# A decoder layer's feed-forwards: a seven-product scheme with other signs, and two of its four weight sums made by transfers that add

## The chip, the cores and the metric

The kernel runs on one core of one Trainium2 chip. The core has a matrix engine (PE), a vector engine (DVE), a scalar engine (ACT), a general engine (POOL) and a queue engine (SP) that starts transfers; each works through its own list of instructions in order, and they wait for one another by semaphores. The metric is device time in microseconds, the median of three runs.

## The reference, cut to what matters

The layer is a chain of a feed-forward, a token mixer (attention beside a convolution), a second feed-forward and a gated embedding. S is 512 tokens, the model width is 1024, the feed-forward's width 2816. What the change touches is `swiglu`, which is called twice:

```
def swiglu(h, w_gu, w_down):
    g, u = jnp.split(h @ w_gu, 2, axis=-1)
    return (jax.nn.silu(g) * u) @ w_down
...
x = x + 0.5 * swiglu(rmsnorm(x, ffn1_norm[i]), ffn1_wgu[i], ffn1_wdown[i])
...
x = x + 0.5 * swiglu(rmsnorm(x, ffn2_norm[i]), ffn2_wgu[i], ffn2_wdown[i])
```

All of it is in 32-bit floats.

## The kernel before, in words

**Products.** Activations are held feature by feature (128 partitions, 512 tokens). Every 32-bit operand is split into a high part (`hi`, made on ACT) and the rest (`lo`, on DVE: source minus high part), and a product is three matmuls (`mm3`): hi times hi, lo times hi, hi times lo. A weight piece is 128x1024 (512 KB).

**Feed-forward.** The 2816 hidden features are 22 columns of 128. The first columns of each feed-forward (4 in the first, 2 in the second, `plain`) are done in the plain way with 512-token matmuls. The other columns are taken two at a time (`pair`): 9 pairs in the first, 10 in the second, 19 in all. A pair is a 2x2 block product (two columns f, two halves kh of the model width, two halves of the tokens), and it is done by a scheme of seven block products instead of eight, once for the gate (g) and once for the up half (u): 14 products of 12 matmuls of 256 tokens. The scheme needs four sums or differences of the token halves, made once for a feed-forward (`sums`, tiles `f_t`), and four sums of the pair's weight blocks (`sm[0]` to `sm[3]`, tiles `f_s`), made for every pair. Blocks are named by f and kh: `A[0,0]`, `A[0,1]`, `A[1,0]`, `A[1,1]`. Each weight sum is two additions of 128x512, so a pair has eight. The products are called in the order 1 and 2, 6 and 5, 7 and 3, 4: 1, 2 and 4 use blocks as loaded, 3, 5, 6 and 7 use sums. After every 8 columns (and at the end) the down projection runs: 8 groups (`f_d`) of 18 or 24 matmuls of 512 tokens. So the pairs stand in six rows: 4 and 6; 8 to 14; 16 to 20 in the first feed-forward, 2 to 6; 8 to 14; 16 to 20 in the second.

**Buffers.** Loaded weights go to 3 buffers (`raw`), and `A[1,1]` to one of 2 more (`k`); high and low parts go to 3 buffers each (`hi`, `lo`). In the first feed-forward (`own`) the high and low parts of a sum have general tiles of their own.

**What sets the order.** The program is first recorded as a list of operations without times. A planner (`costs`, `deadlines`, `simulate`, `plan`) then gives each a cost, walks through them with the buffers it has, and writes one fixed list of instructions for each engine. The additions of the sums are `flex`: the planner puts each on POOL or on DVE. POOL and DVE lock each other out over additions of two tiles (`op.lock`). All instructions are issued by one line (L1522 before), so the profile is read by tile names: `raw_wgu` a loaded piece, `whi_wgu` and `wlo_wgu` its parts, `f_wh` and `f_wl` the parts of a sum with its own tile, `f_s` a sum, `f_g8b`, `f_u8a` the accumulators of pair 8, `f_gs`, `f_us`, `f_gc`, `f_uc` what is read out of them, `f_n_rb` the norm's factor, `f_n_sp` the matmul that makes it.

Of the kernel before, what the change touches and what calls it, by code (L numbers as in the profile page):

```python
# [20 lines left out]
KD = D // P  # L21
# [205 lines left out]
class Program:  # L227
# [69 lines left out]
    def costs(self, op, eng=None):  # L297
# [32 lines left out]
        elif op.what == "dma_start" and eng == "ACT":  # L330
            op.cost, op.lat = 0.5, 2.6
        elif eng == "ACT":
            op.cost, op.lat = 0.07 + n * 0.88e-3, 0.17
            op.cost += 0.094 * vecs
            if "accum_out" in op.k:
                op.cost += 0.1
            f = op.a[2].name if len(op.a) > 2 else "Copy"
            op.fset = SETS.get(f)
        elif eng == "POOL":
            op.lat = 0.15  # L340
            if op.what == "tensor_tensor":
# [25 lines left out]
def deadlines(prog, when):  # L367
# [5 lines left out]
    for op in reversed(prog.ops):  # L373
# [9 lines left out]
        for s in op.succs:  # L383
            d = s.ls
            if s.preds[op] and not s.eng == op.eng == "PE":
                d -= op.lat + (1.8 + op.dma if op.eng == "SP" else 0.0)
            ls = min(ls, d - op.cost)
# [8 lines left out]
def simulate(prog, slots):  # L396
# [64 lines left out]
    def launch(op, t):  # L461
# [19 lines left out]
        if op.eng == "SP":  # L481
            dma_free = max(t + 0.6, dma_free) + op.dma
            op.end = dma_free + 1.5
        else:
            op.end = t + c + op.lat
# [166 lines left out]
def record():  # L652
# [242 lines left out]
    def sums(tag, gain):  # L895
# [4 lines left out]
        t1, t2 = slice(0, HS), slice(HS, S)  # L900
        forms = [[] for _ in range(4)]
        for q in range(KD // 4):
            vs = [ftile(f"{tag}_t{f}_{q}") for f in range(4)]
            for j in range(2):
                k, v = 2 * q + j, [t[:, j * HS : (j + 1) * HS] for t in vs]
                g1, g2 = gain[:, k : k + 1], gain[:, k + 4 : k + 5]
                nc.gpsimd.tensor_tensor(v[0], x[k][:, t2], x[k][:, t1], op=ALU.subtract)
                nc.scalar.activation(v[0], v[0], AF.Copy, scale=g1)
                nc.scalar.activation(v[2], x[k][:, t2], AF.Copy, scale=g1)
                for to, xs, less in ((2, t2, 2), (1, t2, 0), (3, t1, 1)):  # L910
                    nc.vector.scalar_tensor_tensor(
                        v[to], x[k + 4][:, xs], g2, v[less], op0=ALU.mult, op1=ALU.subtract
                    )
# [6 lines left out]
    def ffn(tag, wgu, wdown, h, gain, ss, after, cuts, wide, plain, own):  # L920
# [8 lines left out]

        def act_split(i, u):  # L930
            c, q = i // CH, i % CH // 4
            if (c, q) not in quads:
                quads[c, q] = [nc.tile(f"{tag}_a{c}{q}{p}", [P, 4, S], F32R, "o") for p in "hl"]
            acts[i] = [t[:, i % 4] for t in quads[c, q]]
            split_into(acts[i][0], acts[i][1], u)

# [29 lines left out]
        def pair(i, T, new):  # L966

            A = {}
            for f in range(2):
                for kh in range(2):  # L970
                    A[f, kh] = nc.tile(f"raw_{wgu}{i}_{f}{kh}", [P, PIECE], F32, "k" if f == kh == 1 else "raw")
            sm = [[ftile(f"{tag}_s{n}_{i}_{c}") for c in range(2)] for n in range(4)]

# [4 lines left out]

            def add(n, a, b, op):
                for c in range(2):  # L980
                    s = slice(c * S, (c + 1) * S)
                    ab = [v[c] if isinstance(v, list) else v[:, s] for v in (a, b)]
                    nc.flex.tensor_tensor(sm[n][c], *ab, op=op)

# [17 lines left out]
            for f, kh in ((0, 0), (0, 1), (1, 0), (1, 1)):  # L1002
                load(f, kh)
            add(0, A[1, 0], A[1, 1], ALU.add)
            add(1, sm[0], A[0, 0], ALU.subtract)
            add(3, A[0, 1], sm[1], ALU.subtract)
            add(2, A[0, 0], A[1, 0], ALU.subtract)
            quarter = lambda k0, t: [(h[k][0][:, t], h[k][1][:, t]) for k in range(k0, k0 + 4)]
# [15 lines left out]
            def both(n1, s1, r1, n2, s2, r2, first):  # L1024
                w1, w2 = form(n1, s1), form(n2, s2)
                for m in range(2):
                    times(m, n1, w1, r1, b2, first)
# [3 lines left out]
            for m in both(1, A[0, 0], quarter(0, lo_), 2, A[0, 1], quarter(4, lo_), True):  # L1031
# [3 lines left out]
                if m == 0:  # L1035
                    nc.vector.tensor_tensor(to, to if new else b1[m], rb[:, lo_], op=ALU.mult)
            for m in both(6, sm[1], T[1], 5, sm[0], T[0], False):
                nc.scalar.copy(U[m][:, lo_], b2[m])
                nc.scalar.copy(U[m][:, hi_], b1[m])
            for m in both(7, sm[2], T[2], 3, sm[3], quarter(4, hi_), False):  # L1040
                nc.vector.tensor_tensor((g, u)[m][1][:, hi_], b2[m], U[m][:, hi_], op=ALU.add)
# [11 lines left out]
            nc.vector.tensor_tensor(g[1][:, lo_], b2[0], rb[:, lo_], op=ALU.mult)  # L1053
            nc.scalar.activation(g[1], g[1], AF.Silu)
            nc.vector.tensor_tensor(u[1][:, hi_], u[1][:, hi_], g[1][:, hi_], op=ALU.mult)
            nc.vector.tensor_tensor(u[1][:, lo_], b2[1], g[1][:, lo_], op=ALU.mult)
            act_split(i + 1, u[1])

# [563 lines left out]
```

## Time and profile before

| | |
|---|---|
| three runs | 1172.52, 1174.57, 1174.89 us; median 1174.57 |
| the profiled execution, first to last instruction (span) | 1172.4 us |
| PE busy | 1161.6 us, 99% of the span, granted clock 0.999 |
| DVE, ACT, POOL busy | 973.4, 639.7, 456.2 us |
| HBM read | 112.04 MB |

The profile is of one execution, whose own time the page gives as its span; the median of the runs is 2.2 us above it. Its page has the busy time of each engine, the span in 40 slices, the chain of work that ended last, and groups of instructions with what their engine waited for just before. In a group `out<-in`, the number after x is how many, then the sum, the mean in ns and the idle time before. Where a query gives windows or tiles, times are in us from the span's start.

### The profile page before, as it was taken

To read this page: it belongs to the slowest core of one execution; us is meant where nothing else is said; L and a number is where in the kernel's file an instruction comes from. 1 tells how busy PE (TensorE), PEld (TensorE's weight loads), DVE (VectorE), ACT (ScalarE), POOL (GpSimd) and SP (SyncE) were. 2 spreads that over 40 slices of the span, in tenths; PEclk is the share of its full clock that TensorE was granted. 3 is DMA by queue.
4 is the path that set the end of the run, shared out by engine and by line. 5 is a ranking of instruction groups with operands and counts; after the bars stand their busy time and mean duration, and the time that the engine had idled before them with its cause. 6 is when DMAs were issued, how large, how long until landed. Compare 5 with 4: busy or idle time off the path is not lost.

```text
span 1172.4 us, 17962 instructions
## 1 busy us (share of the span) xinstructions
PE 1161.6 (99%) x6740; PEld 1029.6 (88%) x6740; DVE 973.4 (83%) x1481; ACT 639.7 (55%) x1139; POOL 456.2 (39%) x418
## 2 busy tenths in 40 slices
PE   9999999999999999999999999999999999999998
PEld 7898899889988888878888888889988999899886
DVE  8995799679886898999999786678966997599885
ACT  8552455335545579979865573545541555245542
POOL 2430465033303987887898600104402440122000
PEclk9999999999999999999999999999999999999999
DMA  7422323342233221312223233332333223331331
GB/s 226 146 85 96 126 75 106 99 136 76 82 104 100 90 91 37 108 55 72 76 89 106 88 94 93 105 96 102 107 104 132 74 86 100 121 127 41 104 108 72
DMA packets 37815, 115.30 MB, mean 98 GB/s; under 512 B 4704, under 2 KB 9440, under 8 KB 37728
## 3 DMA queue, kind: packets, MB, share of 16 engines
q1 hardware_dynamic: 37584, 114.12, 31.0%
q8 instruction: 53, 0.87, 0.3%
q14 instruction: 34, 0.28, 0.1%
q10 hardware_dynamic: 144, 0.03, 0.0%
HBM read 112.04 MB, written 2.10 MB: 97 GB/s over the span
## 4 chain that ended last, share of the span: by engine, by line
PE 94%; ACT 2%; DVE 2%; POOL 1%; issue 1%; DMA 0%; SPq 0%; DVEq 0%; ACTq 0%
PE f_d L1522 20%; PE ap L1522 4%; PE ga L1522 4%; PE pg L1522 4%; PE cp L1522 4%; PE wo L1522 4%; PE ca L1522 3%; PE gb L1522 3%; PE cb L1522 3%; PE f_u L1522 2%; PE f_g L1522 2%; PE q1b L1522 2%; PE q0b L1522 2%; PE sc L1522 2%; PE f_u14b L1522 1%; PE f_u20b L1522 1%
## 5 line engine op out<-in xcount | busy, mean ns | idle before, releaser
L1522 POOL TENSOR_TENSOR f_s<-raw_wgu,raw_wgu 128x512 f32<-128x512 f32 x51 | 86.6, 1710 | 345.5 <-DMA raw_wgu<-in_wgu 115.6
L1522 POOL TENSOR_TENSOR y<-y,ct 128x507 f32<-128x507 f32 (+27 forms) x90 | 119.1, 1343 | 6.2 <-ACT ct L1522 4.6
L1522 ACT ACTIVATE whi_wgu<-raw_wgu 128x1024 fp32r<-128x1024 f32 (+1 forms) x93 | 76.2, 834 | 81.5 <-PE f_d L1522 29.5
L1522 DVE TENSOR_TENSOR wlo_wgu<-raw_wgu,whi_wgu 128x1024 fp32r<-128x1024 f32 (+1 forms) x93 | 105.1, 1140 | 7.8 <-ACT whi_wgu L1522 7.3
L1522 DVE SCALAR_TENSOR_TENSOR cz<-u,dww,cz 128x504 f32<-128x504 f32 (+25 forms) x145 | 104.7, 732 | 2.3
L1522 ACT ACTIVATE whi_wd<-raw_wd 128x1024 fp32r<-128x1024 f32 (+1 forms) x48 | 47.4, 987 | 103.9 <-PE f_d L1522 84.6
L1522 DVE TENSOR_TENSOR f_d<-f_d,f_n_rb 128x512 f32<-128x512 f32 x48 | 33.4, 697 | 75.8 <-PE f_d L1522 75.8
L1522 DVE TENSOR_TENSOR f_wl<-f_s,f_wh 128x512 fp32r<-128x512 f32 x72 | 71.4, 1012 | 1.5 <-ACT f_wh L1522 1.0
L1522 POOL TENSOR_TENSOR f_s<-raw_wgu,f_s 128x512 f32<-128x512 f32 x31 | 52.3, 1694 | 51.6 <-DVE f_us L1522 20.6
L1522 DVE TENSOR_TENSOR wlo_wgu<-f_s,whi_wgu 128x512 fp32r<-128x512 f32 x80 | 66.3, 863 | 6.0 <-ACT whi_wgu L1522 5.8
L1522 ACT ACTIVATE whi_wgu<-f_s 128x512 fp32r<-128x512 f32 x80 | 46.6, 625 | 32.4 <-PE f_d L1522 8.9
L1522 ACT ACTIVATE ct<-u,dww 128x505 f32<-128x505 f32 (+28 forms) x90 | 58.2, 701 | 2.2 <-DVE u L1522 2.1
L1522 ACT ACTIVATE f_wh<-f_s 128x512 fp32r<-128x512 f32 x72 | 43.6, 626 | 26.6 <-DVE f_s L1522 12.9
L1522 POOL TENSOR_TENSOR f_s<-f_s,raw_wgu 128x512 f32<-128x512 f32 x31 | 49.2, 1594 | 20.8 <-DVE f_s L1522 6.0
L1522 DVE TENSOR_TENSOR wlo_wd<-raw_wd,whi_wd 128x1024 fp32r<-128x1024 f32 (+1 forms) x48 | 54.1, 1128 | 3.8 <-ACT whi_wd L1522 3.6
L1522 ACT ACTIVATE f_gs<-f_gs 128x512 f32<-128x512 f32 x44 | 27.6, 629 | 34.8 <-DVE f_gs L1522 34.4
L1522 POOL TENSOR_TENSOR f_t<-x 128x256 f32<-128x256 f32 x8 | 6.5, 807 | 86.8 <-DVE x L1522 81.6
L1522 DVE SCALAR_TENSOR_TENSOR x<-f_d,x 128x512 f32<-128x512 f32 x48 | 32.9, 689 | 1.4
L1522 DVE TENSOR_TENSOR f_s<-raw_wgu,raw_wgu 128x512 f32<-128x512 f32 x25 | 32.9, 1319 | 0.0
L1522 ACT ACTIVATE s<-s,m,q_r 128x128 f32<-128x128 f32 x64 | 31.0, 491 | 0.5 <-DVE m L1522 0.4
L1522 ACT ACTIVATE whi_wzc<-raw_wzc 128x1024 fp32r<-128x1024 f32 x16 | 17.0, 1061 | 22.3 <-issue 8.4
L1522 ACT ACTIVATE whi_wzg<-raw_wzg 128x1024 fp32r<-128x1024 f32 x16 | 17.1, 1069 | 16.9 <-PE ga L1522 5.0
(1621 smaller groups left out, 4525.3 us busy)
## 6 DMA issues: line engine op xcount, KB each, us to landing
raw_wgu<-in_wgu SPq DMA_DIRECT2D x80, 512.0 KB, 3.7
raw_wd<-in_wd SPq DMA_DIRECT2D x32, 512.0 KB, 3.5
raw_wzc<-in_wzc SPq DMA_DIRECT2D x16, 512.0 KB, 3.6
raw_wzg<-in_wzg SPq DMA_DIRECT2D x16, 512.0 KB, 3.6
raw_wd<-in_wd SPq DMA_DIRECT2D x16, 384.0 KB, 3.1
raw_wgu<-in_wgu SPq DMA_DIRECT2D x32, 128.0 KB, 2.9
raw_wq<-in_wq SPq DMA_DIRECT2D x8, 512.0 KB, 3.6
raw_wap<-in_wap SPq DMA_DIRECT2D x8, 512.0 KB, 3.6
```

What stands on the lines that cost most here:

```text
L1522: getattr(engines[op.eng], op.what)(*a, **k)
```

## The change

The scheme of seven products is written with other signs, so that every sum of weights is an addition. Two of a pair's four sums are then made by a transfer from HBM that adds to what lies in the buffer (`landed`): `A[1,0]` has `A[1,1]` added to it, and later, when product 1 has its parts and the first sum has been read, `A[0,0]` has `A[1,0]` added to it from HBM. Products 5 and 7 take their parts from these buffers whole. The two sums that stay (`sm[1]`, `sm[3]`) are additions on POOL or DVE as before. The signs of the token sums change with it (two small new operations on POOL hold the negated gain), and the second column of a pair comes out negated, which the scale of its Silu and of its split undo.

```diff
+ADD_ISSUE, ADD_RATE = 1.2, 120e3
...
+        elif eng == "POOL" and op.what == "dma_start":
+            op.cost, op.lat, op.lock = ADD_ISSUE, 0.0, False
+            v = op.writes[0]
+            op.dma = v.free() * v.shape[0] * 4 / ADD_RATE
...
+        less_g = small(f"{tag}_less", 4)
+        nc.gpsimd.tensor_scalar(less_g, gain[:, 4:KD], -1.0, 0.0, op0=ALU.mult, op1=ALU.add)
...
-                nc.gpsimd.tensor_tensor(v[0], x[k][:, t2], x[k][:, t1], op=ALU.subtract)
+                nc.gpsimd.tensor_tensor(v[0], x[k][:, t1], x[k][:, t2], op=ALU.subtract)
...
-            sm = [[ftile(f"{tag}_s{n}_{i}_{c}") for c in range(2)] for n in range(4)]
+            sm = {n: [ftile(f"{tag}_s{n}_{i}_{c}") for c in range(2)] for n in (1, 3)}
...
+            def landed(t, f, kh):
+                nc.gpsimd.dma_start(t, Dram(wgu)[2 * (i + f) + kh], accum_op=ALU.add)
...
-            add(0, A[1, 0], A[1, 1], ALU.add)
-            add(1, sm[0], A[0, 0], ALU.subtract)
-            add(3, A[0, 1], sm[1], ALU.subtract)
-            add(2, A[0, 0], A[1, 0], ALU.subtract)
+            landed(A[1, 0], 1, 1)
+            add(1, A[1, 0], A[0, 0])
+            add(3, A[0, 1], sm[1])
...
             def both(n1, s1, r1, n2, s2, r2, first):
                 w1, w2 = form(n1, s1), form(n2, s2)
+                if first:
+                    landed(A[0, 0], 1, 0)
...
-            for m in both(6, sm[1], T[1], 5, sm[0], T[0], False):
+            for m in both(6, sm[1], T[1], 5, A[1, 0], T[0], False):
...
-            for m in both(7, sm[2], T[2], 3, sm[3], quarter(4, hi_), False):
+            for m in both(7, A[0, 0], T[2], 3, sm[3], quarter(4, hi_), False):
...
-            nc.scalar.activation(g[1], g[1], AF.Silu)
+            nc.scalar.activation(g[1], g[1], AF.Silu, scale=-1.0)
...
-            act_split(i + 1, u[1])
+            act_split(i + 1, u[1], -1.0)
```

The planner writes all lists anew. PE's list has the same 6707 matmuls; within pairs some products change places. The additions of sums fall from 152 (113 on POOL, 39 on DVE) to 76 (50 and 26), and 38 adding transfers come onto POOL's list. In the mixer the lists of DVE, ACT and PE read as before. In the rows below the names are whole: `f1` and `f2` are the feed-forwards, `f1_s3_10_0` is sum 3 of pair 10, first half, and `raw_wgu110_01` is block (0,1) of pair 10 of `wgu1`.

ACT, end of the plain columns of the first feed-forward, before: the conversion for product 1 of pair 4 stands ahead of the copy that makes `f1_n_rb`.

```order
L1522 ACTIVATE whi_wgu17_501<-raw_wgu17_400 128x256 x4
L1522 ACTIVATE f1_t2_1_h_530<-f1_t2_1_189 128x512
L1522 ACTIVATE f1_t3_0_h_548<-f1_t3_0_534 128x512
L1522 ACTIVATE f1_t3_1_h_557<-f1_t3_1_545 128x512
L1522 ACTIVATE whi_wgu14_1_560<-raw_wgu14_00_451 128x1024
L1522 COPY f1_n_rb_564<-f1_n_sp_553 128x512
L1522 ACTIVATE f1_gs0_574<-f1_gs0_574 128x512
```

The same place now:

```order
L1536 ACTIVATE f1_t3_0_h_545<-f1_t3_0_528 128x512
L1536 ACTIVATE whi_wgu17_504<-raw_wgu17_450 128x256
L1536 ACTIVATE f1_t3_1_h_556<-f1_t3_1_539 128x512
L1536 COPY f1_n_rb_567<-f1_n_sp_559 128x512
L1536 ACTIVATE whi_wgu14_5_569<-raw_wgu14_10_404 128x1024
L1536 ACTIVATE f1_wh6_4_1_583<-f1_s1_4_1_573 128x512
L1536 ACTIVATE f1_gs0_579<-f1_gs0_579 128x512
```

The copy now stands ahead of any conversion for pair 4, and the conversion behind it is that of product 5, which reads a buffer that an adding transfer fills.

ACT, the first pair of the second feed-forward (pair 2), before: two conversions of halves of sum 1 stand between the copy of `f2_n_rb` and the table load for Silu.

```order
L1522 ACTIVATE whi_wgu22_5_8249<-f2_s0_2_0_8196 128x512
L1522 COPY f2_n_rb_8256<-f2_n_sp_8244 128x512
L1522 ACTIVATE whi_wgu22_5_8249<-f2_s0_2_1_8202 128x512
L1522 ACTIVATE whi_wgu22_6_8291<-f2_s1_2_0_8215 128x512
L1522 ACTIVATE whi_wgu22_6_8291<-f2_s1_2_1_8220 128x512
L1522 ACT_TABLE_LOAD
L1522 ACTIVATE f2_gs0_8294<-f2_gs0_8294 128x512
L1522 COPY f2_gs2_8314<-f2_g2a_8287 128x256
```

The same place now:

```order
L1536 ACTIVATE whi_wgu22_6_8117<-f2_s1_2_0_8021 128x512
L1536 COPY f2_n_rb_8124<-f2_n_sp_8112 128x512
L1536 ACTIVATE whi_wgu22_6_8117<-f2_s1_2_1_8029 128x512
L1536 ACT_TABLE_LOAD
L1536 ACTIVATE f2_gs0_8139<-f2_gs0_8139 128x512
L1536 COPY f2_gs2_8162<-f2_g2a_8141 128x256
L1536 ACTIVATE f2_gs1_8154<-f2_gs1_8154 128x512
L1536 ACTIVATE f2_a00h_8174<-f2_gs0_8139 128x512
L1536 ACTIVATE whi_wgu22_5_8183<-raw_wgu22_10_7913 128x1024
```

One half of sum 1 is left there, and the conversion of product 5 has moved behind the read of `f2_g2a`.

POOL, the sums of pair 10, before:

```order
L1522 TENSOR_TENSOR f1_s0_10_0_1617<-raw_wgu110_10_1535,raw_wgu110_11_1433 128x512
L1522 TENSOR_TENSOR f1_s2_10_0_1643<-raw_wgu110_00_1484,raw_wgu110_10_1535 128x512
L1522 TENSOR_TENSOR f1_s1_10_1_1686<-f1_s0_10_1_1629,raw_wgu110_00_1484 128x512
L1522 TENSOR_TENSOR f1_s2_10_1_1706<-raw_wgu110_00_1484,raw_wgu110_10_1535 128x512
L1522 TENSOR_TENSOR f1_s3_10_0_1723<-raw_wgu110_01_1493,f1_s1_10_0_1652 128x512
L1522 TENSOR_TENSOR f1_s3_10_1_1770<-raw_wgu110_01_1493,f1_s1_10_1_1686 128x512
```

The same place now (DMA rows are adding transfers):

```order
L1536 DMA raw_wgu110_10_1444<-in_wgu1 128x1024
L1536 TENSOR_TENSOR f1_s1_10_0_1596<-raw_wgu110_10_1444,raw_wgu110_00_1494 128x512
L1536 DMA raw_wgu110_00_1494<-in_wgu1 128x1024
L1536 TENSOR_TENSOR f1_s3_10_0_1655<-raw_wgu110_01_1547,f1_s1_10_0_1596 128x512
L1536 DMA raw_wgu112_10_1699<-in_wgu1 128x1024
```

Six additions have become two transfers and two additions; the other halves of sums 1 and 3 are on DVE, ahead of the read-out of pair 8 and of `wlo_wgu110_1`. SP now loads (1,0) first of a pair's four blocks; that of pair 10 goes into the buffer that (0,1) of pair 8 held.

More of the change, by code (lines that the diff above doesn't have):

```diff
@@ L385, in deadlines @@
             if s.preds[op] and not s.eng == op.eng == "PE":
-                d -= op.lat + (1.8 + op.dma if op.eng == "SP" else 0.0)
+                d -= op.lat + (1.8 + op.dma if op.dma else 0.0)
             ls = min(ls, d - op.cost)
@@ L483, in launch @@
             op.end = dma_free + 1.5
+        elif op.dma:
+            dma_free = max(t + c, dma_free) + op.dma
+            op.end = dma_free + 2.0
         else:
@@ L905, in sums @@
                 k, v = 2 * q + j, [t[:, j * HS : (j + 1) * HS] for t in vs]
-                g1, g2 = gain[:, k : k + 1], gain[:, k + 4 : k + 5]
-                nc.gpsimd.tensor_tensor(v[0], x[k][:, t2], x[k][:, t1], op=ALU.subtract)
+                g1, g2, n2 = gain[:, k : k + 1], gain[:, k + 4 : k + 5], less_g[:, k : k + 1]
+                nc.gpsimd.tensor_tensor(v[0], x[k][:, t1], x[k][:, t2], op=ALU.subtract)
                 nc.scalar.activation(v[0], v[0], AF.Copy, scale=g1)
                 nc.scalar.activation(v[2], x[k][:, t2], AF.Copy, scale=g1)
-                for to, xs, less in ((2, t2, 2), (1, t2, 0), (3, t1, 1)):
+                for to, xs, g, less in ((2, t2, g2, 2), (1, t2, n2, 0), (3, t1, n2, 1)):
                     nc.vector.scalar_tensor_tensor(
-                        v[to], x[k + 4][:, xs], g2, v[less], op0=ALU.mult, op1=ALU.subtract
+                        v[to], x[k + 4][:, xs], g, v[less], op0=ALU.mult, op1=ALU.subtract
                     )
@@ L928, in ffn, with act_split @@
         acts, quads = {}, {}
-        def act_split(i, u):
+        def act_split(i, u, sign=None):
             c, q = i // CH, i % CH // 4
@@ L934, in act_split @@
             acts[i] = [t[:, i % 4] for t in quads[c, q]]
-            split_into(acts[i][0], acts[i][1], u)
+            split_into(acts[i][0], acts[i][1], u, sign)
         ws, gu = {}, {}
@@ L977, in load, with add @@
                 nc.behind = None
-            def add(n, a, b, op):
+            def landed(t, f, kh):
+                nc.gpsimd.dma_start(t, Dram(wgu)[2 * (i + f) + kh], accum_op=ALU.add)
+            def add(n, a, b):
                 for c in range(2):
@@ L982, in add @@
                     ab = [v[c] if isinstance(v, list) else v[:, s] for v in (a, b)]
-                    nc.flex.tensor_tensor(sm[n][c], *ab, op=op)
+                    nc.flex.tensor_tensor(sm[n][c], *ab, op=ALU.add)
             def form(n, src):
```

## The prediction

> **What bounds the kernel now.** I read the page first, for the share of each engine and the chain that ended last, then PE's waits, then windows over the six rows of pairs.
>
> ```profile
> span 1172.4 us, 17962 instructions
> PE 1161.6 (99%) x6740; PEld 1029.6 (88%) x6740; DVE 973.4 (83%) x1481; ACT 639.7 (55%) x1139; POOL 456.2 (39%) x418
> PE 94%; ACT 2%; DVE 2%; POOL 1%; issue 1%; DMA 0%; SPq 0%; DVEq 0%; ACTq 0%
> ```
>
> ```profile
> PE sc L1522 <- DVE qT_l L1522: 2.0, 1, 2.0
> PE warm L1522 <- DVE ones L1522: 1.1, 1, 1.1
> PE f_u L1522 <- ACT f_n_rb L1522: 0.7, 1, 0.7
> PE f_g2a L1522 <- ACT f_gs L1522: 0.6, 1, 0.6
> PE ple_sp L1522 <- DVE ple_dgl L1522: 0.6, 1, 0.6
> ```
>
> PE is busy 99% of the span, and its five largest waits come to 5.0 us (the numbers added). A busy PE need not be at its peak, so its pace has to be seen: one product of a pair is 12 matmuls in 1.44 us, and the chain of waits shows them end to end. In the windows (PE, PEld, DVE, ACT, POOL busy, clock, share of the DMA engines, GB/s) PE has no hole in the row of pairs 8 to 14 of the first feed-forward, 0.62 us in the first row of the second and 0.08 us in the next.
>
> ```profile
> 136.70 1.43 PE f_g8b L1522 x12
> 138.13 1.44 PE f_g8a L1522 x12
> ...
> 155.41 1.44 PE f_u8b L1522 x12
> 156.85 1.44 PE f_g10b L1522 x12
> ```
>
> ```profile
> 138.10:217.50 79.40, 79.40 (x662) 79.30 (x661) 74.77 (x107) 42.23 (x76) 35.31 (x22) 1.00 0.30 97
> 800.70:862.00 61.30, 60.68 (x505) 60.48 (x504) 55.87 (x84) 38.09 (x68) 21.38 (x13) 1.00 0.26 85
> 905.50:986.50 81.00, 80.92 (x674) 80.72 (x673) 74.53 (x110) 46.43 (x83) 26.84 (x17) 1.00 0.26 84
> ```
>
> So the engines that the change relieves, DVE at 94% (74.77 of 79.40) and POOL at 44%, are not what sets the end of these rows: PE is, and its 6707 matmuls stay. A pair takes 156.85 - 136.70 = 20.15 us whatever DVE does, as long as its parts come in time. The change can win only where PE waits now; it can lose wherever a sum comes late.
>
> **The additions that go.** 63 fewer on POOL, 13 fewer on DVE:
>
> ```profile
> L1522 POOL TENSOR_TENSOR f_s<-raw_wgu,raw_wgu x51: 1282/1741/2284, 42.4 to 1057.1; 128x512 f32<-128x512 f32 x51
> L1522 DVE TENSOR_TENSOR f_s<-raw_wgu,raw_wgu x25: 676/1771/1789, 44.2 to 1070.4; 128x512 f32<-128x512 f32 x25
> L1522 DVE TENSOR_TENSOR wlo_wgu<-raw_wgu,whi_wgu x93: 408/1214/2320, 5.4 to 1083.0; 128x1024 fp32r<-128x1024 f32 x61, 128x256 fp32r<-128x256 f32 x32
> ```
>
> (shortest, median, longest in ns). That is 63 x 1.74 = 110 us off POOL and 13 x 1.77 = 23 us off DVE, and more on DVE, whose additions take 676 ns alone and 1771 beside one of POOL's. On the path that ends the rows it is worth 0, since PE covers it; without that cover, DVE's 94% says it would be worth much. The parts of sums 0 and 2, until now two operations of 128x512 each, become one of 128x1024 where they had tiles of their own: less work again, worth 0 for the same reason.
>
> **First place where PE waits: the copy of f_n_rb.** Three rows in order of time (the loads of the last plain piece, its conversions, the last token part), then the chain:
>
> ```profile
> 26.34 2.22 SPq L1522 DMA_DIRECT2D raw_wgu<-in_wgu  x5
> 35.14 1.34 ACT L1522 ACTIVATE whi_wgu<-raw_wgu 128x256 fp32r<-128x256 f32 x4 [2.19 <-PE f_u L1522]
> 40.24 0.63 ACT L1522 ACTIVATE f_t_h<-f_t 128x512 fp32r<-128x512 f32 x1 [0.16 <-DVE f_t L1522]
> ```
>
> ```profile
> 40.49 0.24 PE f_n_sp L1522
> 40.74 0.04 issue
> 40.77 1.04 ACT whi_wgu L1522
> 41.82 0.48 ACT f_n_rb L1522
> 42.30 0.04 issue
> 42.34 0.97 PE f_u L1522 x3
> ```
>
> The 1.04 us of the conversion stand between PE's last matmul and the copy that PE waits for. In the new list the copy comes first. What is ahead of it on ACT is the last token part (f_t, sum 3): before, it ran from 40.24 for 0.63 us, and its inputs on DVE come in nearly the same order, so the copy is free to start at 40.77. The last plain piece (raw_wgu17), loaded at 26.34, comes after (1,0) of pair 4 now, but its conversions wait for PE to free a buffer until 35.14 anyway. Gain between 0 (ACT is late by the same) and 1.04; I take 1.0, since only this conversion is ahead.
>
> **Second place: the read-out of f_g2a.**
>
> ```profile
> 801.43 0.54 ACT whi_wgu L1522
> 801.97 1.65 issue
> 803.62 1.15 ACT whi_wgu L1522 x2
> 804.79 1.28 ACT L1522
> 806.07 0.01 issue
> 806.09 0.90 ACT f_gs L1522 x2
> 806.98 0.04 issue
> 807.03 1.70 PE f_g2a L1522 x12
> ```
>
> PE stands for 0.6 us and then starts slowly (1.70 for 1.44): 0.9 in all. Ahead of the table load (1.28) stood a pause and two conversions, 2.8 us, which have gone behind. The table load can end at 801.97 + 1.28 = 803.3 and the read-out just after PE has made f_g2a, at about 803.9; PE needs it at 806.4. Next in line is product 5: its conversion stands behind two operations of 0.6 us on ACT, so about 805.5 to 806.6, and its low part takes 1.2 us on DVE behind another of 0.7: 808.0 to 808.3, against 807.9 when PE wants it. That gives back 0.1 to 0.4. Gain between 0 and 0.9; I take 0.5.
>
> **The adding transfers.** No row shows one. They carry 512 KB, like a load:
>
> ```profile
> raw_wgu<-in_wgu SPq DMA_DIRECT2D x80, 512.0 KB, 3.7
> DMA packets 37815, 115.30 MB, mean 98 GB/s; under 512 B 4704, under 2 KB 9440, under 8 KB 37728
> ```
>
> Let L be the time from POOL starting one until its sum has landed. Lower bound 3.7 us, a plain load. Upper bound: the buffer's old content has to be fetched as well, so twice 3.7, plus an issue by POOL of the order of one of its own additions (1.74) and one DVE operation that may be in the way (2.32): 11.5. I take 2 x 3.7 + 1.7 = 9.1, as the row nearest to the work (512 KB moved twice). The 38 bring 38 x 0.524 = 20 MB more from HBM; in the rows of pairs the DMA engines are busy 0.26 to 0.30, and half as much again (three transfers for two in a pair) plus the fetch leaves them under two thirds.
>
> What waits behind one: on POOL the next addition, on DVE the other half of sum 1, and behind that, in order, the read-out of the pair before and the low part of product 1. Follow pair 10. Its (1,0) is loaded into the buffer of (0,1) of pair 8, which is free when sum 3 of pair 8 has read it; then load (3.7), adding transfer (L), sum 1 (1.7), sum 3 (1.7), and the buffer is free for the next pair. This ring must close within a pair: 3.7 + L + 1.7 + 1.7 = 7.1 + L against 20.15, so it holds up to L = 13.0. For the second transfer, product 7 needs its parts 8 products after product 1 starts (11.5 us), 2.3 us of conversion before that; the transfer may start when the low part of product 1 is made, several us ahead of it: L up to about 12 again. With L = 9.1, or at its upper bound, PE does not wait, and the 38 cost 0. The first pairs of most rows load under a down projection:
>
> ```profile
> 93.16 43.55 PE f_d L1522 x192
> ```
>
> that is 43.55 us in which only 8 pieces are converted.
>
> **Small things.**
>
> ```profile
> 19.73 0.19 POOL L1522 TENSOR_SCALAR sinks_n<-sinks 128x16 f32<-128x16 f32 x1
> ```
>
> The two new operations on POOL for the negated gain are of the size of the one for the sinks (0.19 us) and hold up the first f_t by 0.3 us at most, which ACT covers by doing the other token form first: 0, bound 0.3.
>
> **A rule that speaks against it.** DVE is busy 94% of the row at 138 us, and an addition on it is stretched from 676 to 1771 ns when POOL is at one: the two lock each other out. The Trainium skill, page "SBUF — State Buffer", section "SBUF: two separate sides", warns that a DMA issued from GpSimd has its descriptors written by GpSimd's cores, and that while VectorE runs an operation in a two-port mode these are locked out and the transfer seems stuck. It says also that an operation with two SBUF inputs is in the way only of a GpSimd operation that reads SBUF, and DVE's list here is mostly such operations, so I give the rule a minority of the chance (rival 1).
>
> **The sum.** 1172.4 - 1.0 - 0.5 + 0 = 1170.9 for the span; the median of the runs lies 2.2 above the span of the profiled execution, so 1173.1.
>
> **Rivals.**
> 1. *Starved or slow adding transfers*: slower. L passes 13.0 because POOL's issue has to fit between DVE's operations. Then every pair that follows another in its row is longer by L - 13.0; there are 13 such (19 less the six first ones). At L = 14, 13 x 1.0 = 13 us, 1186; at 15, 26 us, 1199. For it: DVE's 94%, and the stretched additions. Against it: 13.0 is 3.5 times a load, and DVE gets 23 us and more of relief. It decides from L = 13; below that nothing is seen.
> 2. *All of PE's small waits go*: faster. 1.04 and 0.9 in full, and the 2.0 us of `sc` behind DVE's qT_l, 3.9 us in all: 1170.6. For it: everything after 42 us is earlier by 1 us. Against it: the lists in the mixer are unchanged and move as a whole, so the 2.0 should stay.
> 3. *The gains are given back in place* (product 5 late at both places, ACT waiting for a transfer): no change, 1174.6. For it: at the first place the operation behind the copy is the conversion of product 5, which waits for a transfer; against it: its load is issued where the last plain piece's was, at 26 to 27 us, and even L = 11.5 lands it before 43, when ACT gets there.
>
> **Numbers.** A measurement of this kernel tells 0.2% (2.3 us) from no change. My forecast holds 0.40, rival 3 0.17, rival 1 0.25, rival 2 0.18. The forecast and rival 3 lie within 0.2%, except for the part of the forecast that comes out a us better: faster 0.21, same 0.54, slower 0.25. The range goes from rival 2 (1170.6, rounded down for scatter) to rival 1 at L = 14: 1170 to 1187.
>
> **What would show it.** Right: PE waits for f_n_rb of 0.7 and f_g2a of 0.6 gone, windows of the rows of pairs without holes, DVE under 90% there, adding transfers that land in 9 us. Wrong: POOL's sums or DVE's f_s idle for adding transfers with PE holes in second and later pairs; L over 13; or f_g2a replaced by a wait for wlo_wgu of product 5.

## The result, and the profile after

The changed kernel takes 1183.41 us in the median (1181.2 to 1185.95), the kernel before, run beside it, 1174.59. The ratio is 1.0079, with an interval of 1.0058 to 1.0101: slower, by 8.8 us. I had forecast 1173.1.

The profiled execution, from its page:

```profile
span 1184.2 us, 17782 instructions
PE 1165.5 (98%) x6740; PEld 1030.8 (87%) x6740; DVE 912.8 (77%) x1430; ACT 636.0 (54%) x1101; POOL 376.4 (32%) x395
PE 87%; DVE 9%; ACT 2%; issue 2%; DMA 0%; SPq 0%; DVEq 0%; ACTq 0%
```

The relief came: DVE is busy 61 us less than before, POOL 80 us less. But the chain that ended last now runs over DVE for 9% of the span (2% before). PE's waits say where (total, times, longest, in us):

```profile
PE f_g14a L1536 <- DVE wlo_wgu L1536: 2.7, 1, 2.7
PE sc L1536 <- DVE qT_l L1536: 2.1, 1, 2.1
PE f_g4a L1536 <- DVE wlo_wgu L1536: 1.4, 2, 1.2
PE f_g12a L1536 <- DVE wlo_wgu L1536: 1.2, 1, 1.2
...
PE f_g6a L1536 <- DVE wlo_wgu L1536: 1.1, 1, 1.1
PE f_g20a L1536 <- DVE wlo_wgu L1536: 0.9, 1, 0.9
PE f_g10a L1536 <- DVE wlo_wgu L1536: 0.7, 1, 0.7
...
PE f_u L1536 <- ACT f_n_rb L1536: 0.2, 1, 0.2
```

Six rows that were not there, seven waits, 8.0 us, and all of one kind: PE has done both halves of product 1 of a pair and stands for the low part of product 2's weights, block (0,1). (Accumulator a takes products 2, 5 and 3, accumulator b products 1, 6, 7 and 4.) After such a wait the first product also runs slowly, 1.69 us for 1.44.

By stage, from the start of PE's first matmul in each:

| us | before | after |
|---|---|---|
| start and plain products, to pair 4 | 52.7 | 52.2 |
| the 19 pairs (19 x 20.155 = 382.95 is their floor) | 384.35 | 393.78 |
| down projections | 239.5 | 239.5 |
| mixer | 423.3 | 426.05 |
| plain products of the second feed-forward | 23.2 | 23.2 |
| end | 49.4 | 49.5 |

The pairs hold 9.4 us of it. The mixer's 2.7 are not the change's: the same lists took 421.8 in another run below.

What stood in the pairs otherwise, in the rows of pairs 8 to 14 of each feed-forward (the first window is that of before; the second is longer, for the row now ends at 997) and in the group of the new transfers (issues with the median time to landing; then shortest, median and longest issue in ns; then landing):

```profile
138.10:217.50 79.40, 78.71 (x654) 78.36 (x654) 60.99 (x92) 42.39 (x69) 16.04 (x13) 1.00 0.54 140
905.50:997.00 91.50, 87.62 (x702) 86.10 (x701) 67.48 (x99) 46.04 (x75) 22.06 (x17) 1.00 0.52 129
```

```profile
raw_wgu<-in_wgu SPq DMA_DIRECT2D x80, 512.0 KB, 4.4
raw_wgu<-in_wgu POOLq DMA_DIRECT2D x38, 512.0 KB, 5.6
L1536 POOL DMA_DIRECT2D raw_wgu<-in_wgu x38: 856/877/1029, 30.8 to 1081.3; - x38
DMA to landing us min/median/max: 5.3/5.6/9.6
```

DVE is down from 94% to 77% of the row at 138 us, and an adding transfer lands in 5.6 us, not in the 9.1 that I had estimated. So the transfers were faster than forecast, DVE was freer, and PE waited all the same.

The largest wait, pair 14 of the second feed-forward, in the chain of waits and then on ACT:

```profile
972.46 1.44 PE f_u12b L1536 x12
973.90 1.44 PE f_g14b L1536 x12
975.34 1.45 PE f_u14b L1536 x12
...
977.14 1.06 ACT whi_wgu L1536
978.20 0.02 issue
978.23 1.24 DVE wlo_wgu L1536
...
979.50 1.69 PE f_g14a L1536 x12
```

```profile
971.05 1.06 ACT L1536 ACTIVATE whi_wgu<-raw_wgu 128x1024 fp32r<-128x1024 f32 x1 [0.19 <-PE f_u12a L1536]
974.02 0.63 ACT L1536 ACTIVATE whi_wgu<-f_s 128x512 fp32r<-128x512 f32 x1 [1.90 <-PE f_u12b L1536]
...
975.08 0.62 ACT L1536 ACTIVATE whi_wgu<-f_s 128x512 fp32r<-128x512 f32 x1
...
977.14 1.06 ACT L1536 ACTIVATE whi_wgu<-raw_wgu 128x1024 fp32r<-128x1024 f32 x1 [0.88 <-PE f_u14b L1536]
```

The conversions are those of product 5 (971.05), of the two halves of sum 1 for product 6 (974.02, 975.08), and only then of product 2 (977.14), which has to wait until PE is done with product 1 (`f_u14b`) to have one of the three buffers for high parts. The list was written so. Over the pairs, ACT's list has the conversions of raw blocks and sums in this order (in the first feed-forward products 3 and 6 have tiles of their own and are left out):

```
second feed-forward, before: 1 2 5 6 7 3 4 (pair 2)   1 2 6 5 7 3 4 (all others)
second feed-forward, after:  pairs 4, 6: 1 6 2 5 3 7 4   12, 20: 1 5 2 6 3 7 4   14: 1 5 6 2 3 7 4
first feed-forward, after:   pair 4: 5 1 2 4 7           10: 1 5 2 7 4
```

These are all the pairs of the changed kernel in which product 2 is not second, seven of 19, and they are the seven with a wait. In the other twelve it is second, and PE doesn't stop for it. The loads are a part of why the list does this. SP loads the blocks of pair 14 in the order (1,1), (0,0), (0,1), (1,0) before, and (1,0), (0,0), (1,1), (0,1) now: the block of product 2 has become the last. It is the last in all seven pairs, but in five of the other twelve too, so this alone doesn't fix the order. Four rows of after (the load of (0,0) for pair 14, the low part of product 7 of pair 12, the load of (0,1) that follows it, the low part of product 7 of pair 14), and three of before (loads of (0,0) and (0,1), and the last addition that reads (0,0)):

```profile
956.38 0.33 SPq L1536 DMA_DIRECT2D raw_wgu<-in_wgu  x1
965.00 1.23 DVE L1536 TENSOR_TENSOR wlo_wgu<-raw_wgu,whi_wgu 128x1024 fp32r<-128x1024 f32 x1 [1.89 <-ACT whi_wgu L1536]
966.25 0.33 SPq L1536 DMA_DIRECT2D raw_wgu<-in_wgu  x1
988.09 1.23 DVE L1536 TENSOR_TENSOR wlo_wgu<-raw_wgu,whi_wgu 128x1024 fp32r<-128x1024 f32 x1 [3.18 <-ACT whi_wgu L1536]
```

```profile
947.49 0.33 SPq L1522 DMA_DIRECT2D raw_wgu<-in_wgu  x1
947.86 0.42 SPq L1522 DMA_DIRECT2D raw_wgu<-in_wgu  x1
962.35 2.28 POOL L1522 TENSOR_TENSOR f_s<-raw_wgu,raw_wgu 128x512 f32<-128x512 f32 x1
```

Before, (0,0) of pair 14 holds its buffer from 947.49 to 964.63, 17.1 us, and is gone before the pair begins (966.2). Now it waits there for the second transfer, then for the conversion of product 7: 956.38 to 989.32, 32.9 us. Three buffers have 3 x 20.15 = 60.5 us for a pair's three blocks. The load of (0,1) waits for (0,0) of the pair before to go (966.23), and comes 7.5 us ahead of product 1; before, 18.3 us. Pair 14 is the extreme of both kernels: over the 19 pairs (0,0) is held for 21.2 us before and 25.9 now in the median, (1,0) for 14.7 and 24.9, and what gives way is (0,1), whose load comes 21.1 us ahead of product 1 before and 11.6 now.

The late load doesn't stop PE directly. In all seven pairs (0,1) had landed 3.4 to 10.0 us before its conversion began (in pair 14 at 969.8, against 977.14). PE waits for the place that the planner, which reckons with 7.6 us for an adding transfer, gave to the conversion.

So theory 1: **held buffers**. An adding transfer turns a raw buffer into the sum's own place, so it is occupied until the sum is converted; three shared buffers are too few for that. Theory 2: the transfers cost by themselves (traffic, POOL's issue, slow landing). Theory 3: the signs and the new token sums cost.

### The profile page after: what moved, and what is told of

It is laid out like the page before. It is cut to its first block, busy times and chain, and to the rows that moved or that the text cites. A ratio compares the mean times of both kernels' runs of the same rounds, so it can differ in the third digit from the quotient of the medians.

```text
span 1184.2 us, 17782 instructions
## 1 busy us (share of the span) xinstructions
PE 1165.5 (98%) x6740; PEld 1030.8 (87%) x6740; DVE 912.8 (77%) x1430; ACT 636.0 (54%) x1101; POOL 376.4 (32%) x395
## 4 chain that ended last, share of the span: by engine, by line
PE 87%; DVE 9%; ACT 2%; issue 2%; DMA 0%; SPq 0%; DVEq 0%; ACTq 0%
PE f_d L1536 20%; PE ap L1536 4%; PE ga L1536 4%; PE pg L1536 4%; PE cp L1536 4%; PE wo L1536 4%; PE cb L1536 3%; PE gb L1536 3%; DVE wlo_wgu L1536 2%; PE ca L1536 2%; DVE cz L1536 2%; PE q1b L1536 2%; PE sc L1536 2%; PE f_g L1536 1%; PE f_u L1536 1%
## 5 line engine op out<-in xcount | busy, mean ns | idle before, releaser
L1536 DVE TENSOR_TENSOR wlo_wgu<-raw_wgu,whi_wgu 128x1024 fp32r<-128x1024 f32 (+1 forms) x131 | 144.0, 1106 | 39.0 <-ACT whi_wgu L1536 38.6
L1536 ACT ACTIVATE whi_wgu<-raw_wgu 128x1024 fp32r<-128x1024 f32 (+1 forms) x131 | 116.4, 898 | 105.9 <-PE f_d L1536 31.7
L1536 POOL DMA_DIRECT2D raw_wgu<-in_wgu x38 | 33.4, 879 | 351.4 <-DMA raw_wgu<-in_wgu 102.7
L1536 POOL TENSOR_TENSOR f_s<-raw_wgu,raw_wgu 128x512 f32<-128x512 f32 x20 | 33.0, 1652 | 125.3 <-DMA raw_wgu<-in_wgu 111.6
L1536 POOL TENSOR_TENSOR f_s<-raw_wgu,f_s 128x512 f32<-128x512 f32 x30 | 45.4, 1522 | 17.0 <-DMA raw_wgu<-in_wgu 14.5
L1536 DVE TENSOR_TENSOR wlo_wgu<-f_s,whi_wgu 128x512 fp32r<-128x512 f32 x40 | 29.9, 782 | 8.1 <-ACT whi_wgu L1536 8.0
L1536 ACT ACTIVATE whi_wgu<-f_s 128x512 fp32r<-128x512 f32 x40 | 23.2, 625 | 21.2 <-PE f_d L1536 8.9
L1536 DVE SCALAR_TENSOR_TENSOR x<-f_d,x 128x512 f32<-128x512 f32 x48 | 32.9, 689 | 1.4
L1536 DVE TENSOR_TENSOR f_wl<-f_s,f_wh 128x512 fp32r<-128x512 f32 x36 | 32.5, 930 | 0.0
L1536 ACT ACTIVATE whi_wzg<-raw_wzg 128x1024 fp32r<-128x1024 f32 x16 | 17.1, 1068 | 16.9 <-PE ga L1536 5.1
L1536 PE MATMUL ca<-mix_h_h,wlo_wzc 128*128 128x512 f32 x64 | 25.4, 397 | 0.0
L1536 PE MATMUL cb<-mix_h_h,wlo_wzc 128*128 128x512 f32 x64 | 25.2, 393 | 0.0
```

The source lines that it names most:

```text
L1536: getattr(engines[op.eng], op.what)(*a, **k)
```

## The experiments

In each, the planner writes its lists anew unless it is said that they are the same. "Start" is the time to pair 4 and "pairs" that of the 19 pairs in the profiled execution, both against before (52.7 and 384.35). The kernel before was run beside each, with medians of 1173.1 to 1176.1 us, so the ratios are to be compared and not the medians.

| | start | pairs | median us | ratio to before, interval |
|---|---|---|---|---|
| the change | -0.5 | +9.4 | 1183.4 | 1.0079 (1.0058 to 1.0101) |
| four sums by additions | +0.6 | -0.2 | 1173.1 | 1.0000 (0.9990 to 1.0009) |
| first transfer alone | -0.1 | +5.0 | 1179.2 | 1.0050 (1.0035 to 1.0064) |
| second transfer alone | +0.6 | +3.6 | 1177.8 | 1.0043 (1.0028 to 1.0057) |
| plain transfers, same lists | 0.0 | +9.9 | 1183.0 | 1.0083 (1.0068 to 1.0098) |
| five buffers in one pool | -0.2 | +1.4 | 1179.4 | 1.0036 (1.0022 to 1.0049) |
| the same in the kernel before | +3.4 | +2.6 | 1180.3 | 1.0046 (1.0028 to 1.0064) |
| list told 6.4 us a transfer | +1.9 | +3.7 | 1179.6 | 1.0036 (1.0024 to 1.0049) |
| five buffers, first transfer alone | +0.3 | +2.9 | 1181.6 | 1.0051 (1.0033 to 1.0068) |
| own buffers for (1,0) | +3.9 | +0.9 | 1179.7 | 1.0042 (1.0025 to 1.0058) |
| the same in the kernel before | +0.3 | +8.4 | 1182.2 | 1.0060 (1.0039 to 1.0081) |
| the same, first transfer alone | +2.0 | +3.1 | 1182.2 | 1.0071 (1.0053 to 1.0089) |
| own for (1,0), first pairs by additions | +0.6 | +0.9 | 1175.0 | 1.0011 (0.9997 to 1.0024) |
| own for (1,0), first pairs' buffers as in the change | 0.0 | +2.7 | 1177.0 | 1.0022 (1.0012 to 1.0032) |
| list told 3 us a transfer | +0.1 | +44.1 | 1221.8 | 1.0407 (1.0392 to 1.0422) |
| first pairs by additions, old buffers | +0.3 | +8.6 | 1181.5 | 1.0066 (1.0050 to 1.0083) |

**Four sums by additions, signs of the change.**

```diff
-            landed(A[1, 0], 1, 1)
-            add(1, A[1, 0], A[0, 0])
+            add(0, A[1, 0], A[1, 1])
+            add(1, sm[0], A[0, 0])
             add(3, A[0, 1], sm[1])
+            add(2, A[0, 0], A[1, 0])
...
-                if first:
-                    landed(A[0, 0], 1, 0)
```

> The signs of the change, but all four sums of a pair made by additions on POOL and DVE, as in the kernel before; no adding transfer. The list converts product 2's weights second in every pair again. Theory 1 (held buffers: the adding transfers keep two of the three raw buffers for most of a pair, so the piece of product 2 is loaded last, the list converts products 5 and 6 ahead of it, and PE stops for product 2's low part at seven pairs): 1172 to 1175 us, none of the seven waits of PE for wlo_wgu inside the pairs. Theory 2 (the adding transfer costs by itself: slow landing, traffic, descriptors): 1172 to 1175 as well. Theory 3 (the new signs and the tokens' new forms cost): stays at 1181 to 1186.

1173.1, no difference. Theory 3 falls. PE's waits are those of before, the two that I had expected to go among them:

```profile
PE f_u L1535 <- ACT f_n_rb L1535: 0.7, 1, 0.7
PE f_g2a L1535 <- ACT f_gs L1535: 0.6, 1, 0.6
```

So these two are a matter of where the lists with transfers put ACT's conversions, not of the signs.

**Plain transfers, the lists unchanged.**

```diff
-                nc.gpsimd.dma_start(t, Dram(wgu)[2 * (i + f) + kh], accum_op=ALU.add)
+                nc.gpsimd.dma_start(t, Dram(wgu)[2 * (i + f) + kh])
```

> The changed kernel with the same instructions in the same order on every engine, but the 38 transfers that POOL issues overwrite their buffer instead of adding to it (this leaves the additions of sums 0 and 2 out). Theory 1 (the order of the list and the buffers that it frees): 1180 to 1185, the seven waits for wlo_wgu stay, since they hang on the list. Theory 2 (the adding itself is slow): the transfers land in 3.7 to 4.5 us instead of 5.6 and the time falls to 1174 to 1178.

```profile
raw_wgu<-in_wgu POOLq DMA_DIRECT2D x38, 512.0 KB, 3.8
```

```profile
PE f_g14a L1536 <- DVE wlo_wgu L1536: 2.7, 1, 2.7
PE f_g12a L1536 <- DVE wlo_wgu L1536: 1.4, 1, 1.4
...
PE sc L1536 <- DVE qT_l L1536: 0.4, 1, 0.4
```

The transfers land 1.8 us sooner, and the time is the same 1183.0. Six of the seven waits for product 2 stay, the largest with the same 2.7 us (that of pair 4 of the second feed-forward is gone, and three waits for products 6 and 7 of 0.3 to 0.6 us have come). The adding costs 1.8 us a transfer and nothing in the end. What this run can't exclude is the traffic, which it keeps, and POOL's issue, which it only shortens (0.57 us for 0.88).

**One transfer of the two.** The first alone (sum 2 is then sum 1 less (1,1), by an addition), and the second alone (sum 0 by additions):

```diff
-                if first:
-                    landed(A[0, 0], 1, 0)
...
+            add(2, sm[1], A[1, 1], ALU.subtract)
```

```diff
-            landed(A[1, 0], 1, 1)
-            add(1, A[1, 0], A[0, 0])
+            add(0, A[1, 0], A[1, 1])
+            add(1, sm[0], A[0, 0])
```

> Only the first adding transfer of a pair (sum 0); sum 2 is made by an addition as sum 1 less the piece (1,1). 19 adding transfers instead of 38. The buffer of (0,0) is free again after sum 1 and product 1, so product 2's piece is not last and is converted second in all pairs that follow another. Theory 1: 1171 to 1176, waits only at the first pair of a row, where the list converts product 5 first (pairs 4, 8, 18 of the first feed-forward, 8 of the second), 0 to 1.2 us each. Theory 2 (each adding transfer costs the same): half of the loss stays, about 1179. Theory 3: 1181 to 1186.

> Only the second adding transfer of a pair (sum 2, into the buffer of (0,0)); sum 0 is made by additions, so the buffer of (1,0) is free early. The list converts product 2 second in every pair. Theory 1: none of the waits of product 2, 1172 to 1177; if product 7 comes late after its transfer, a wait for its low part instead. Theory 2: half of the loss stays, about 1179. Theory 3: 1181 to 1186.

1179.2 and 1177.8, half of the loss each, as theory 2 had it and above theory 1's ranges. But the waits are others. With the first alone the longest is for product 5 (1.7 us, pair 2 of the second feed-forward). With the second alone there is none for product 2, and none for product 7 either, for which I had allowed. PE stops before the second half of product 6, in pairs 6, 12, 14 and 20 of the second feed-forward; these are the four pairs in which ACT's list converts product 5 ahead of 6. Two of the four:

```profile
PE f_g12b L1536 <- DVE wlo_wgu L1536: 0.8, 1, 0.8
PE f_g14b L1536 <- DVE wlo_wgu L1536: 0.8, 1, 0.8
```

That the waits move from product to product with the order of the list speaks against a cost for each transfer. These two runs alone don't decide between the theories.

**The buffers.** All four loaded blocks of a pair from one pool of five, the same memory; the two tiles of the mixer that used the old pair of buffers go there too:

```diff
-SLOTS = {"a": 54, "o": 4, "raw": 3, "hi": 3, "lo": 3, "ps": 8, "k": 2, "x": 8, "c": 100000}
+SLOTS = {"a": 54, "o": 4, "raw": 5, "hi": 3, "lo": 3, "ps": 8, "x": 8, "c": 100000}
...
-                    A[f, kh] = nc.tile(f"raw_{wgu}{i}_{f}{kh}", [P, PIECE], F32, "k" if f == kh == 1 else "raw")
+                    A[f, kh] = nc.tile(f"raw_{wgu}{i}_{f}{kh}", [P, PIECE], F32, "raw")
```

> The changed kernel with its raw buffers in one pool: five raw buffers for the four pieces of a pair instead of three for (0,0), (0,1), (1,0) and two of their own for (1,1); the same memory, the same 38 adding transfers, the same traffic. The list converts product 2 second in every pair again. Theory 1 (held buffers): the seven waits for product 2's low part go, the pairs are within 1 to 3 us of 20.15 us each in sum, 1172 to 1176 us. Theory 2 (the transfers cost by themselves: traffic, POOL's issue, landing): 1180 to 1185, since nothing of them is changed.

> The same pooling of the raw buffers in the kernel before, as a control: 5 instead of 3 and 2, nothing else. Theory 1: before has no lack of raw buffers, so no change, 1171 to 1175 us. Theory 2: no change either. If this is faster by as much as the changed kernel gains from it, the pooling is good for another reason and says nothing on the change.

> The first adding transfer alone (sum 2 is sum 1 less the piece (1,1), by an addition) with the five raw buffers in one pool. Theory 1: no buffer is short, product 2 is second everywhere, 1170 to 1174 us, as fast as the kernel before or a little faster. Theory 2 (half of the transfers, half of their cost): 1177 to 1179, as with the first transfer alone and three buffers.

The pairs came back to 1.4 us over before, with all 38 transfers. The total did not: 1179.4, and the kernel before, where I had expected no change, became slower by 0.46%. The pool is also the mixer's, whose lists were written anew, and in the kernel before the start became 3.4 us longer; how much of the rest is the mixer's lists and how much its own spread (below) was not separated. The third of these runs missed its range as well (1181.6). A cleaner step was needed, one that leaves start and mixer alone: (1,0) gets the two buffers of (1,1), which goes to the pool of three.

```diff
-                    A[f, kh] = nc.tile(f"raw_{wgu}{i}_{f}{kh}", [P, PIECE], F32, "k" if f == kh == 1 else "raw")
+                    A[f, kh] = nc.tile(f"raw_{wgu}{i}_{f}{kh}", [P, PIECE], F32, "k" if (f, kh) == (1, 0) else "raw")
```

> The changed kernel with one word moved: the piece (1,0), which the first adding transfer adds into, now has the two buffers that were (1,1)'s, and (1,1) goes into the pool of three. The same memory, the same 38 adding transfers, the same traffic; startup and mixer keep their three buffers. The list converts product 2 second in all 19 pairs. Theory 1 (held buffers): no wait for product 2's low part in the pairs that follow another; the 19 pairs sum to within 3 us of 19 x 20.15 = 382.9 us (the changed kernel: 10.8 over); 1170 to 1175 us. Theory 2 (the transfers cost by themselves): 1180 to 1185.

> The same word moved in the kernel before, as a control. There (1,0) is read by sums 0 and 2 and is free early, while (1,1) is held from its load until product 4, at the end of the pair, so it is now (1,1) that blocks the pool of three. Theory 1 (which piece is held long decides who may share): slower than before, 1175 to 1182 us, with waits in the second feed-forward where the list takes product 7 ahead of 5. If it is faster by 2 us or more, the place of the buffers is better in itself and the gain of the changed kernel from it is no evidence.

> The first adding transfer alone (sum 2 by an addition), with the two buffers of (1,1) given to (1,0). Theory 1: product 2 is second in all pairs and no piece is late: 1170 to 1175 us, as the changed kernel with the same buffers. Theory 2 (each transfer costs the same): 1177 to 1179.

The same place as above, pair 14 of the second feed-forward, in the chain of waits of the changed kernel with (1,0) in its own buffers:

```profile
973.85 1.44 PE f_g14b L1536 x12
975.29 1.44 PE f_g14a L1536 x12
976.73 1.44 PE f_u14b L1536 x12
```

Product 2 follows product 1 at once. All 38 transfers, the same traffic and the same issues on POOL, and the pairs are 0.9 us over before instead of 9.4: theory 2 falls. (What is left in the pairs is two waits for product 5, of 1.0 and 0.7 us.) The control goes the other way: in the kernel before, the same word costs 8.4 us in the pairs, with (1,1), which is held till the end of a pair, now in the pool of three. The time is 1179.7 still, out of the range that I had given, because the start became 3.9 us longer (`f_u`). The mixer of this execution was 2.8 longer than that of before too (`sc`), as in the changed kernel:

```profile
PE f_u L1536 <- ACT f_n_rb L1536: 2.5, 1, 2.5
PE sc L1536 <- DVE qT_l L1536: 2.1, 1, 2.1
...
PE f_g2a L1536 <- DVE wlo_wgu L1536: 1.0, 1, 1.0
```

POOL's additions for pair 4 now stand beside DVE's token sums, ahead of the copy that `f_n_rb` is, and ACT converts product 1 of pair 4 ahead of that copy again; the next runs take them away from there. The run with the first transfer alone missed: sum 2 reads (1,1) there and holds it, in the shared pool. That this is why is argued, not shown.

**Start and buffers apart.** Pair 4 of the first and pair 2 of the second feed-forward keep their additions, all others have the transfers (34 of 38), once with (1,0) in its own buffers in these others, once with the buffers of the change:

```diff
+            plain = (tag, i) in (("f1", 4), ("f2", 2))
...
+            if plain:
+                add(0, A[1, 0], A[1, 1])
+                add(2, A[0, 0], A[1, 0])
+            else:
+                landed(A[1, 0], 1, 1)
...
-                if first:
+                if first and not plain:
                     landed(A[0, 0], 1, 0)
```

> As the run that gave (1,0) the two buffers of its own, but the first pair of each feed-forward (4 of the first, 2 of the second) is left as it was: its sums made by additions, (1,1) in the two buffers of its own. 34 of the 38 adding transfers stay, all in pairs that begin after a pair or a down projection. That run lost 4.0 us before its first pair, where POOL's first transfer and additions stood beside DVE's token parts, and 1.2 us in pair 2 of the second feed-forward. Theory 1 (held buffers, with the startup as a second cost): startup within 1 us of the kernel before's, pairs within 2 us of 382.9 in sum, 1171 to 1175 us. Theory 2 (each transfer costs the same): 1181 to 1184, as 34 of 38 are still there.

> The counterpart of the run with the first pairs of each feed-forward by additions: the same 34 adding transfers and the same additions in pairs 4 and 2, but the buffers are those of the changed kernel ((1,1) in its own two, (1,0) in the pool of three). Five of the seven pairs keep product 2 behind 5 or 6 in the list (10 of the first feed-forward; 6, 12, 14, 20 of the second). Theory 1: their waits stay, 1179 to 1183 us, against 1175.0 with (1,0) in its own buffers. If it is at 1175 too, the first pairs' transfers were the loss, and the buffers nothing.

PE's waits inside the pairs, of the first and then of the second:

```profile
PE f_g2b L1542 <- DVE f_gs L1542: 1.1, 1, 1.1
...
PE f_g12a L1542 <- DVE wlo_wgu L1542: 0.7, 1, 0.7
```

```profile
PE f_g14a L1542 <- DVE wlo_wgu L1542: 2.5, 1, 2.5
...
PE f_g12a L1542 <- DVE wlo_wgu L1542: 1.0, 1, 1.0
...
PE f_g10a L1542 <- DVE wlo_wgu L1542: 0.7, 1, 0.7
...
PE f_g6a L1542 <- DVE wlo_wgu L1542: 0.5, 1, 0.5
PE f_g20a L1542 <- DVE wlo_wgu L1542: 0.5, 1, 0.5
```

1175.0 and 1181.5, with the same operations. The first can't be told from the kernel before (1.0011, 0.9997 to 1.0024); its time is at the top of its range, and its pairs are 2.4 us over 382.9, where I had expected 2. Its two waits are for products 6 and 5. The second has most of the loss. In the second the list puts product 5 or 6 ahead of 2 in five pairs, and PE waits there in all five. This is the pair of runs that settles it between the two theories: with the planner told the same, which block shares a buffer with which decides, not the transfers.

A third run left all 38 transfers and gave pairs 4 and 2 the buffers of the change:

```diff
-                    A[f, kh] = nc.tile(f"raw_{wgu}{i}_{f}{kh}", [P, PIECE], F32, "k" if (f, kh) == (1, 0) else "raw")
+                    A[f, kh] = nc.tile(f"raw_{wgu}{i}_{f}{kh}", [P, PIECE], F32, "k" if (f, kh) == ((1, 1) if (tag, i) in (("f1", 4), ("f2", 2)) else (1, 0)) else "raw")
```

> As the run that gave (1,0) the two buffers of its own, but in the first pair of each feed-forward (4 of the first, 2 of the second) the buffers are those of the changed kernel: (1,1) in its own two, (1,0) in the pool of three; all 38 adding transfers. In pair 4 the list still converts product 5 ahead of 1 and 2, as in the changed kernel. Theory 1: startup as in the changed kernel (47.1 us of plain products, against 47.6 before and 51.6 in that run), pair 4 1 to 1.5 us over 20.15, the other pairs within 2 us in sum: 1172 to 1176 us. Theory 2: 1181 to 1185.

1177.0, a little over the range. The start is as before, pair 4 has its wait (1.2 us, then 0.25 of slow start), as expected. The other pairs are 2.6 us over their floor, where I had expected 2, with PE waiting for product 5 in three of them.

**What the planner is told.** The transfers took less than the 7.6 us that it was told (1.2 + 4.4 + 2.0). Told 0.9 + 3.5 + 2.0, and told 0.5 + 0.5 + 2.0:

```diff
-ADD_ISSUE, ADD_RATE = 1.2, 120e3
+ADD_ISSUE, ADD_RATE = 0.9, 150e3
```

```diff
-ADD_ISSUE, ADD_RATE = 1.2, 120e3
+ADD_ISSUE, ADD_RATE = 0.5, 1e6
```

> The changed kernel, but the planner that makes the lists is told what the trace shows of an adding transfer: 0.9 us of issue and 3.5 us of moving before it lands (it was told 1.2 and 4.4). The transfers themselves are the same. Four of the seven pairs keep product 2 behind product 5 or 6 in the list (4 of the first feed-forward; 4, 12, 20 of the second). Theory 1: about four of the seven waits stay, 1176 to 1181 us. Theory 2: 1180 to 1185.

> The changed kernel, its buffers and its 38 adding transfers as they are, but the planner is told that one takes 0.5 us of issue and lands 2.5 us later, half of what the trace shows (5.6). The list then loads (0,0) and (0,1) of a pair first and (1,0) last, and converts product 2 second in every pair. Theory 1a (three buffers are truly too few for pieces held this long): the waits move from product 2 to products 5 and 6, whose sums come late on the chip; 1178 to 1184 us. Theory 1b (the buffers suffice; the loss is the place that the planner gave product 2's piece, because it was told 7.6 us for a transfer): no waits of over 0.5 us in the pairs that follow another, 1173 to 1177 us. Theory 2 (the transfers cost by themselves): 1181 to 1185.

With the figure nearer to the truth most of the loss in the pairs goes, on the buffers of the change (3.7 over before instead of 9.4; three waits for product 2 stay), and the start is 1.9 longer. So the buffers are not all of the cause: they left so little room that the planner's wrong figure moved product 2 back. With too little told, product 2 is second everywhere, and at 1221.8 it is far worse, outside every range that I had given. ACT, in pair 12 of the second feed-forward:

```profile
989.99 1.06 ACT L1536 ACTIVATE whi_wgu<-raw_wgu 128x1024 fp32r<-128x1024 f32 x1 [7.68 <-DMA raw_wgu<-in_wgu]
```

```profile
PE f_g12b L1536 <- ACT f_gc L1536: 5.0, 1, 5.0
PE f_g6b L1536 <- ACT f_gc L1536: 4.3, 1, 4.3
```

ACT stands 7.7 us for a transfer whose block the list converts too early, with the read-outs that PE needs behind it. So moving product 2 forward in the list is not enough on these buffers; something else is late then. As a proof of too few buffers this run is weak, since here the wait is for a landing that the planner was told wrongly; the two runs with 34 transfers carry it.

No variant beat both kernels. The pairs' floor is only 1.4 us below what the kernel before takes, and no run's pairs were more than 0.2 below the kernel before's.

## Why the prediction was wrong

**What bounds the kernel**: right. PE is at its pace except where a part comes late, and 61 us less on DVE and 80 less on POOL are worth nothing by themselves.

**f_n_rb**, 1.0 forecast (0 to 1.04): PE's wait fell from 0.7 to 0.2, the start by 0.5. **f_g2a**, 0.5 forecast: the wait is gone, pair 2 went from 21.03 to 20.25 us, 0.8. Both right in kind. Together 1.3 for 1.5; that the sum is so near is luck, for one came out at half and the other above its figure.

**The transfer's time**: L was estimated at 9.1, between 3.7 and 11.5; it landed in 5.6. An error to the safe side in the ring that I worked out, but not in the lists: the planner was told 7.6, and told 6.4 it gave lists that lose 3.7 us in the pairs instead of 9.4.

**The step that failed** is the next one: "Follow pair 10. Its (1,0) is loaded into the buffer of (0,1) of pair 8 ... so it holds up to L = 13.0", and from it "PE does not wait, and the 38 cost 0". I followed one buffer round its ring and asked only how long the transfer may take. I did not follow the block that a transfer adds into to its last reader. (1,0) has to stay until product 5 is converted (24.9 us in the median pair instead of 14.7) and (0,0) until product 7 is (25.9 instead of 21.2; in pair 14 32.9 instead of 17.1), and that delays the load of whatever comes next into such a buffer: (0,1). With blocks of three kinds in three buffers, the rings are not apart, and they were nearly full before (58.1 us of holds in the median pair, of 60.5). The planner put product 2 behind 5 or 6 in seven pairs, and the term that I had at 0 measured 9.4 us in the pairs: the place of the loss is the block that did not change at all. The lists that I could read showed it. I quoted SP's loading of (1,0) first, and did not ask which block was now last, nor in which order ACT converts.

**Rival 1** had the right side, and 1183.4 lies in the range that I stretched to it, but by another mechanism. It was to decide from L = 13; at 5.6 the loss was there, and making the transfers 1.8 us faster changed nothing. The page "SBUF — State Buffer" of the Trainium skill, section "SBUF: two separate sides", on descriptors that VectorE keeps GpSimd from writing, was the reason I gave for it: in this kernel the 38 issues took 856 to 1029 ns each, and the slowest transfer landed in 9.6 us, so none came near the 13 at which I had the rival decide. The page's own exception, that an operation with two SBUF inputs is in the way only of a GpSimd operation that reads SBUF, agrees with that; no run here tests it.

**Of what I said would show it**, the two waits went (0.2 us is left at `f_n_rb`), DVE was under 90% and all transfers but one (9.6) landed within 9 us; the windows without holes did not come. Of the signs of the wrong outcome the first was half right: holes in second and later pairs, but for product 2, not for sums idle behind transfers.

## What to carry to other kernels

When an operation is changed to work in place, list for every buffer of the pool the load and the last reader, before and after; a longer hold shows as a late load of some other block. The sum of the holds says less, since a block that is loaded early holds its buffer too: in the 19 pairs it was 49 to 75 us before and 59 to 74 after. Tell the planner a new operation's cost from a trace as soon as there is one. Read in the new lists which load has become the last and which conversion has moved behind, even for operations that the change doesn't touch. Then give own buffers to what is held longest across a period's edge, and let what is short-lived share: here one word moved took 8.6 of the 9.4 us in the pairs.

## What the runs showed of the hardware

A transfer of 512 KB that adds to its buffer landed in 5.6 us (median), a plain one on the same queue in 3.8. SP's loads of the same blocks landed in 3.7 in the kernel before, in 4.4 beside the adding transfers and in 4.1 beside the plain ones. POOL was busy 0.88 us with each adding issue and 0.57 with a plain one.

The mixer's length is not fixed by its lists: the changed kernel and its variant with plain transfers have the same instructions in the same order on every engine, and their mixers took 426.05 and 421.8 us in the profiled executions, with PE's wait for `qT_l` at 2.1 and 0.4 us in them. That is about the spread of the kernel before (1172.15 to 1177.05 us over all its runs here), and reason to compare stages and not spans. Where it arises can be read, comparing the two executions matmul by matmul: 0.8 us come at `qTp`, with a wait of 0.6, 0.3 just behind it, 1.6 are the longer wait at `sc`, and 1.5 come just after that, where from 510.10 to 514.20 the granted clock was 0.58 in the changed kernel and stayed at 1.00 in the other. In the kernel before a wait of 2.0 us at the same matmul was followed by full speed, so the wait alone doesn't bring this about. What sets it is open.
